# A fifth room for raw weight units, shared with the turning of panels, and four units loaded ahead instead of three, in the MLPs of a two-layer encoder trunk

## The chip, the cores and the metric

The kernel runs on one core of one Trainium2 chip. The metric is device time in microseconds (us) from one launch, the median of several runs; lower is better. The engines are called PE (TensorE, matrix products), ACT (ScalarE), DVE (VectorE), POOL (GpSimd) and SP (SyncE, which here only issues DMAs).

## The reference, cut to what matters

The input x is 256 rows of 2048 floats. Everything is float32. Two layers run one after the other: a layer with causal attention under a forget gate, and a layer with chunked attention on shared keys and values. Each ends in an MLP, and the two MLPs are where the change acts.

```python
def sq_relu_mlp(h, g, w1, w2):
    a = jax.nn.relu(rms_norm(h, g) @ w1)     # w1: 2048 x 8192
    return (a * a) @ w2                      # w2: 8192 x 2048
...
    h = h + o.reshape(B, S, D) @ a_w_out[l]
    h = h + sq_relu_mlp(h, mlp_norm_g[layer], mlp_w1[layer], mlp_w2[layer])
...
kv = rms_norm(h, kv_norm_g) @ kv_w
...
    h = h + o.reshape(B, S, D) @ b_w_out[l]
    h = h + sq_relu_mlp(h, mlp_norm_g[layer], mlp_w1[layer], mlp_w2[layer])
```

## The kernel before

**Products in three passes.** A float32 weight unit of 128 x 1024 is split into two parts that PE takes at its faster format: ACT copies it to `hi` (line 259) and DVE takes `lo = raw - hi` (line 260). The activations are split in the same way. PE then runs three passes over a unit: `hi` with the activations' high part (line 522), `hi` with their low part (line 524), `lo` with their high part (line 526). `hi` and `lo` have three rooms each.

**The loader.** All weight units of the program stand in one deque, `units`, in the order in which they are used. `load()` (line 234) takes the next, gives it a room of the pool `wraw` (four rooms of 128 x 1024, line 93) and issues its DMA of 512 KB on SP (line 242). `issue()` (line 245) takes the oldest loaded unit and writes down its ACT copy and its DVE subtraction. `fetch()` calls `top_up()` (line 274), which keeps two units split ahead of PE (`AHEAD`) and three raw units loaded ahead of the splitting (`EARLY`), and hands the next split unit to the products. So one raw unit loaded follows each raw unit issued, and a load has to wait for the room of the unit loaded four before it, that is, for that unit's `lo`.

**The MLP** is 16 pairs of column blocks in a planned order (`plan_mlp`), blocks of the first product and of the second by turns. A pair of blocks is multiplied by a scheme with seven products of sums of panels in place of eight, over a quarter of the depth for the first pair and over half of it for the 15 others (`deep`). Four panels of a pair (1 MB each in a deep pair) are brought whole by SP (`bring`, line 861). DVE sums some of them (`make`, line 865, its addition at line 879); other sums are made by a DMA of POOL that adds the panel in memory to the panel on the chip (`put`, line 881, its DMA at line 885). A unit made from those panels is called a form; it has no load of its own, passes through the loader's queue as a place holder, and is six matmuls long. A raw unit is twelve matmuls long. A deep pair has 14 forms and 8 raw units; the first pair has 7 forms, 12 raw units and four panels of 512 KB. `prepare` (line 887) decides how many units before a pair each of its panels is brought and summed.

**The turning of panels.** A finished panel of the hidden layer must be turned before it is an operand of the second product. DVE turns its 32 x 32 blocks from the accumulator into a room `z` (`blocks32`, line 369, its instruction at line 372). From there the blocks go to their places either by 16 small DMAs from chip to chip, eight on SP and eight on POOL (`hop`, line 392), or through memory with one DMA out (`turn<-z`, line 382) and four back (line 388; `carry`, line 375). The panels of the residual stream that feed the next normalisation go through `z` as well. `z` comes from the pool `qkv` with two rooms of 128 x 1024 (line 403 in `turned`, two being the pool's number). These z rooms are as large as a room for a raw unit.

**Order.** What is to be done a few units after an event waits in a list, `fill`, of which `run_fill()` takes one place after a unit. At the end `keep_order` (line 70) binds DVE, ACT, PE and SP to the written order; POOL's order is left to the scheduler. So a DMA of SP that waits holds up every later DMA of SP.

Of the kernel before, what the change touches and what calls it, by code (L numbers as in the profile page):

```python
# [9 lines left out]
F32 = mybir.dt.float32  # L10
# [5 lines left out]
P = 128  # L16
# [11 lines left out]
UN = 1024  # L28
# [53 lines left out]
def trunk(ctx: ExitStack, tc: tile.TileContext, xT, xr, gs, hg, bf, wgate, w_in, w_oa, w1a, w1fa, w1sa, w2fa, w2sa,  # L82
# [4 lines left out]
    def pool(name, bufs, **kw):  # L87
        return ctx.enter_context(tc.tile_pool(name=name, bufs=bufs, **kw))
# [4 lines left out]
    wraw = pool("wraw", 4)  # L93
    qkv = pool("qkv", 2)
# [36 lines left out]
    units = deque()  # L131
# [99 lines left out]

    raws = deque()

    def load(parts=1, queue=SY):
        src = units.popleft()
        if isinstance(src, Form):
            raws.append((src, ()))
            return
        raw = wraw.tile([P, UN], F32, name="raw")
        n = UN // parts  # L240
        cuts = [slice(i * n, (i + 1) * n) for i in range(parts)]
        queue.dma_start(raw, src)
        raws.append((raw, cuts))

    def issue(parts=1):
        form = None
        if not raws:
            load(parts)
        raw, cuts = raws.popleft()
        if not cuts:  # L250
            form, half = raw, raw.half
            raw, cuts = form.pair.t[form.name], [slice(0, form.pair.cols - UN if half else UN)]
            if half:
                raw = raw[:, UN:]
        n = cuts[-1].stop
        hi = wsp.tile([P, n], F32R, name="hi" if n == UN else "hih", bufs=3 if n == UN else 1)
        lo = wsp.tile([P, n], F32R, name="lo" if n == UN else "loh", bufs=3 if n == UN else 1)
        for c in cuts:
            S.activation(hi[:, c], raw[:, c], AF.Copy)  # L259
            V.tensor_tensor(lo[:, c], raw[:, c], hi[:, c].bitcast(F32), op=ALU.subtract)  # L260
        ready.append((hi, lo, n < UN))
        if form and form.pair.deep and form.name == "T3":
            make(form.pair, "T2", int(half))
        elif form and half == form.pair.wide:
            if form.name == "T3":
                make(form.pair, "T2")
            elif form.name == "T2" and form.pair.adds:
                put(form.pair, "T4")

    def half_next():  # L270
        u = raws[0][0] if raws else units[0]
        return isinstance(u, Form) and u.half and not u.pair.deep

    def top_up(ahead=AHEAD, early=EARLY):
        while (units or raws) and sum(1 for r in ready if not r[2]) <= ahead and not (half_next() and any(r[2] for r in ready)):
            issue()
        while units and sum(1 for r in raws if r[1]) < early:
            load()

    def fetch(ahead=AHEAD, early=EARLY):  # L280
# [14 lines left out]
    turns = [0]  # L295
# [45 lines left out]
    def room(tag, name, dtype=F32):  # L341
        return qkv.tile([P, DEEP], dtype, name=name, tag=tag, bufs=1)
# [17 lines left out]
    def steps(make):  # L360
        box = []

        def step():
            if not box:
                box.append(make())
            next(box[0])
        return step
# [34 lines left out]
    def turned(name=None):  # L402
        z = qkv.tile([P, GH * T], F32, name="z")
        return (z, qkv.tile([P, GH * T], F32, name=name, tag=name, bufs=2)) if name else z
# [361 lines left out]
    early = room("bias", "early")  # L766
# [127 lines left out]
                (bring if name[0] != "T" else put if p.adds and name == "T1" else make)(p, name)  # L894

    def mlp(plan, x, Sx, st, last, more=None):
        base = turns[0]
        hids = [[] for _ in range(NCH)]
        Sh = [[] for _ in range(NCH)]

        def take(t, c, n):
            S.activation(t, t, AF.Relu)
            y = acts.tile([P, 2, GH, T], F32R, name="act")
            hi, lo = (y[:, i].rearrange("p k (b i c) -> p (k b) i c", b=NB, i=4) for i in range(2))
            t3 = t.rearrange("p (i kb c) -> p kb i c", i=4, c=32)
            yield
            S.activation(hi, t3, AF.Square)
            yield
            S.activation(t, t, AF.Square)
            yield  # L910

            def low():
                V.tensor_tensor(lo, t3, hi.bitcast(F32), op=ALU.subtract)

            hids[c].extend(y[:, :, j, :] for j in range(GH))
            low()
            yield
            if n == 0:
                r = prob.tile([P, 4 * UN], F32R, name="Sh", tag="p", bufs=1)
                Sh[c].extend(r[:, i : i + n] for i, n in ((0, UN), (UN, UN), (2 * UN, UN), (3 * UN, UN)))  # L920
                yield from sums([[t3[:, 2 * j + b :: 4] for j in range(2)] for b in range(NB)], Sh[c])
            elif n == 1:
                yield from sums([[t3[:, 2 * j + b :: 4] for j in range(2)] for b in range(NB)], Sh[c][2:])

        def turn_hidden(c, n):
            zt = []

            def f(b, ps):
                if b == 0:
                    zt.extend(turned("q"))  # L930
                blocks32(ps, zt[0], b)
                if b == NB - 1:
                    step = steps(lambda: take(zt[1], c, n))
                    at = TURNS[c > 0][n]
                    way = [hop(*zt)[0][0]] if at[1] < 0 else [i[0] for i in carry(*zt, 0)[:2]]
                    items = [[] for _ in range(max(at) + 1)]
                    for i, d in zip([i for i in at if i >= 0], way + [step] * (len(at) - 2)):
                        items[i].append(d)
                    add_fill(items)
            return f  # L940

        def open_pair(p):
            second, c, r = p.at
            if c < NCH:
                p.x, p.fs = (hids[c], Sh[c]) if second else (x, Sx)
            p.ps = [acc_pair(base), acc_pair(2 if p.third else 1 - base)]
            if c == NCH:
                p.x, p.fs, evacs = more
                p.evac = evacs[2 * r : 2 * r + 2]
            elif second:  # L950
                p.evac = [(last if c == NCH - 1 else residual)(2 * r + q, st.r2) for q in range(2)]
            else:
                p.evac = [turn_hidden(c, 2 * r + q) for q in range(2)]

        starts = [i for i, it in enumerate(plan) if it[1:] == (2, 0)]
        for i, (p, q, u) in enumerate(plan):
            hi, lo = ready.popleft()[:2] if q > 1 and ready and not p.deep else fetch()
            if p.ps is None:
                open_pair(p)
            f, kind, k = plan[i - 1]  # L960
            done = k if i and kind > 1 and kind == 2 + f.wide else None
            if q > 1:
                form_products(p.ps, hi, lo, p.x, p.fs, u, q == 3, p)
                if u == 1 and q == 2 + p.wide:
                    p.t["P7"] = wk.tile([P, 512], F32, name="p7", tag="wk")
                    S.activation(p.t["P7"], p.ps[1][0], AF.Copy)
                elif u == 2 and q == 2 + p.wide:
                    V.scalar_tensor_tensor(p.ps[0][1], p.ps[1][0], -1.0, p.t["P7"], op0=ALU.mult, op1=ALU.subtract)
                if q == 2 + p.wide:
                    if not p.deep:  # L970
                        top_up(AHEAD - 1)
                    if u == 1:
                        S.activation(p.ps[1][0], p.ps[1][1], AF.Copy, scale=-1.0)
                    if p.deep:
                        run_fill()
            else:
                products(p.ps[q], hi, lo, p.x, u, not units and not ready, p.fast)
                if p.fast and (q, u) == (0, p.own):
                    V.tensor_tensor(p.ps[1][1], p.ps[1][0], p.t["P7"], op=ALU.add)
                run_fill()  # L980
                if u == KT // UA - 1:
                    for b in range(NB):
                        p.evac[q](b, p.ps[q][b])
                nxt = next((j for j in starts if j > i), None)
                if nxt is not None:
                    d = sum(1 for it in plan[i:nxt] if it[1] < 2)
                    prepare(plan[nxt][0], d)
            if done == 1 and not f.adds:
                make(f, "T4")
            elif done == 2:  # L990
                S.activation(f.ps[0][0], f.ps[1][1], AF.Copy)
# [20 lines left out]
    for g in range(NG):  # L1012
# [8 lines left out]
                add_fill([[]] * (9 if g else 7) + [[lambda: qs.append(scale_q(box["lq"], 1, g))]])  # L1021
        evs.append(f)
    mlp(plan_a, x1, S1, st1, next_b, (xb, Sb, evs))
    st2f = st2.flipped

    def rel_bias(g, box):
# [116 lines left out]
```

## Time and profile before

| | |
|---|---|
| median of 3 runs | 2078.71 us (2078.18 to 2079.30) |
| the profiled execution's own time | 2078.09 us |
| its span, first to last instruction | 2076.2 us |
| granted TensorE clock | 1.000 |
| PE busy | 2062.0 us, 99% |
| DVE busy | 1712.5 us, 82% |
| ACT busy | 1313.2 us, 63% |
| POOL busy | 222.9 us, 11% |
| DMA | 543.08 MB, mean 262 GB/s |

The profile is of one execution. Its span lies 1.9 us under that execution's own time. Times inside it are counted from the span's start. Busy is the union of an engine's instructions; matmuls overlap one another in it, since each is given from its start to a modelled end. "A <- B" means that A waited and that B ended last of what it waited for. The first MLP lies at about 400 to 1034 us, the second from about 1405 us to the end; between them are the query, key and value products and the second attention.

### The profile page before, as it was taken

The numbers are of one execution on the slowest core, as the hardware profiler recorded it, in microseconds if no ns is written. First come the engines' busy times: TensorE is split into PE (matmuls) and PEld (weight loads), VectorE is DVE, ScalarE is ACT, GpSimd is POOL, SyncE is SP. The second block draws the span as 40 slices with busy tenths as digits, with TensorE's granted clock in tenths as the row PEclk, the third lists the DMA queues.
The fourth block names the chain that finished last, engine by engine and source line by source line (L and its number), as shares of the span: only waits on it lengthen the run. The fifth ranks groups of instructions, "written<-read, shape, count | busy, mean of one in ns | idle before, by whom it ended". The sixth has DMA issues, their size and how long they took to land.

```text
span 2076.2 us, 26893 instructions
## 1 busy us (share of the span) xinstructions
PE 2062.0 (99%) x9140; PEld 1702.9 (82%) x9140; DVE 1712.5 (82%) x1974; ACT 1313.2 (63%) x1587; POOL 222.9 (11%) x339
## 2 busy tenths in 40 slices
PE   9999999999999999999999999999999999999999
PEld 8888888878878888888878888887788888888887
DVE  6767666799899899899988577768998988998996
ACT  6544444777667677677776445456766776766764
POOL 1111000021101102101011001000211111011020
PEclk9999999999999999999999999999999999999999
DMA  7787778788888898898888777787888888888985
GB/s 287 250 256 237 231 257 263 270 255 270 292 252 279 262 291 281 241 293 271 259 252 273 233 231 237 233 274 270 271 269 278 250 283 288 269 278 258 297 249 174
DMA packets 170682, 543.08 MB, mean 262 GB/s; under 512 B 40480, under 2 KB 68528, under 8 KB 147504
## 3 DMA queue, kind: packets, MB, share of 16 engines
q1 hardware_dynamic: 153008, 463.16, 62.9%
q0 software_dynamic: 17248, 77.64, 18.7%
q8 instruction: 72, 1.18, 0.2%
q10 hardware_dynamic: 288, 0.57, 0.1%
q14 instruction: 66, 0.54, 0.1%
HBM read 501.39 MB, written 26.24 MB: 254 GB/s over the span
## 4 chain that ended last, share of the span: by engine, by line
PE 95%; DMA 3%; ACT 1%; DVE 1%; issue 0%; POOL 0%; ACTq 0%; DVEq 0%; SPq 0%; POOLq 0%
PE acc L526 25%; PE acc L524 25%; PE acc L522 25%; PE s L522 6%; PE s L524 6%; PE s L526 6%; PE s L666 1%; PE po L696 1%; DMA raw<-in_w2sa 1%; DMA wT<-in_w1fa 1%; DMA raw<-in_w2sb 1%; DMA raw<-in_w1b 0%; DMA query<-turn 0%; ACT hi L259 0%; PE po L697 0%; PE s L665 0%
## 5 line engine op out<-in xcount | busy, mean ns | idle before, releaser
L260 DVE TENSOR_TENSOR lo<-raw,hi 128x1024 fp32r<-128x1024 f32 (+1 forms) x514 | 619.7, 1211 | 184.7 <-ACT hi L259 171.3
L259 ACT ACTIVATE hi<-raw 128x1024 fp32r<-128x1024 f32 (+1 forms) x514 | 540.4, 1054 | 341.4 <-PE acc L524 251.4
L522 PE MATMUL acc<-hi,act 128*128 128x512 f32 x2076 | 578.3, 394 | 5.4 <-ACT hi L259 3.4
L526 PE MATMUL acc<-lo,act 128*128 128x512 f32 x2076 | 569.6, 389 | 0.1
L524 PE MATMUL acc<-hi,act 128*128 128x512 f32 x2076 | 569.2, 389 | 0.1
L522 PEld LDWEIGHTS acc<-hi,act 128*128 128x128 f32 x2076 | 387.4, 188 | 85.4 <-ACT hi L259 4.5
L526 PEld LDWEIGHTS acc<-lo,act 128*128 128x128 f32 x2076 | 388.7, 188 | 83.7 <-DVE lo L260 3.4
L524 PEld LDWEIGHTS acc<-hi,act 128*128 128x128 f32 x2076 | 389.4, 188 | 82.6 <-DVE act L353 1.3
L259 ACT ACTIVATE hi<-w 128x1024 fp32r<-128x1024 f32 x258 | 271.1, 1058 | 120.9 <-PE acc L524 105.5
L260 DVE TENSOR_TENSOR lo<-w,hi 128x1024 fp32r<-128x1024 f32 x258 | 310.0, 1217 | 17.4 <-ACT hi L259 16.4
L260 DVE TENSOR_TENSOR lo<-wT,hi 128x1024 fp32r<-128x1024 f32 x184 | 223.2, 1221 | 51.0 <-ACT hi L259 47.5
L259 ACT ACTIVATE hi<-wT 128x1024 fp32r<-128x1024 f32 x184 | 193.3, 1059 | 88.6 <-PE acc L524 34.6
L398 POOL DMA_DIRECT2D q<-z x208 | 103.6, 510 | 259.9 <-DVE z L372 209.6
L522 PE MATMUL s<-hi,act 128*128 128x512 f32 x358 | 98.8, 391 | 3.1 <-ACT hi L259 2.6
L526 PE MATMUL s<-lo,act 128*128 128x512 f32 x358 | 98.6, 390 | 0.0
L524 PE MATMUL s<-hi,act 128*128 128x512 f32 x358 | 98.2, 389 | 0.0
L522 PEld LDWEIGHTS s<-hi,act 128*128 128x128 f32 x358 | 66.8, 188 | 18.4 <-ACT hi L259 3.9
L526 PEld LDWEIGHTS s<-lo,act 128*128 128x128 f32 x358 | 66.9, 188 | 14.6 <-DVE lo L260 0.9
L524 PEld LDWEIGHTS s<-hi,act 128*128 128x128 f32 x358 | 67.2, 188 | 14.1
L879 DVE TENSOR_TENSOR wT<-wT,w 128x1024 f32<-128x1024 f32 x62 | 75.9, 1225 | 2.1
L879 DVE TENSOR_TENSOR wT<-w,w 128x1024 f32<-128x1024 f32 x62 | 75.2, 1214 | 0.3
L608 POOL TENSOR_TENSOR ss<-ss,mhalf 128x4 f32<-128x4 f32 x32 | 43.2, 1357 | 271.0 <-DVE ss L607 270.9
(181 smaller groups left out, 1819.6 us busy)
## 6 DMA issues: line engine op xcount, KB each, us to landing
raw<-in_w_in SPq DMA_DIRECT2D x95, 512.0 KB, 4.5
w<-in_w2fa SPq DMA_DIRECT2D x32, 1024.0 KB, 7.3
raw<-in_w2sa SPq DMA_DIRECT2D x64, 512.0 KB, 6.9
raw<-in_w_kv SPq DMA_DIRECT2D x64, 512.0 KB, 4.4
w<-in_w2fb SPq DMA_DIRECT2D x32, 1024.0 KB, 7.1
raw<-in_w2sb SPq DMA_DIRECT2D x64, 512.0 KB, 6.8
w<-in_w1fa SPq DMA_DIRECT2D x28, 1024.0 KB, 7.4
raw<-in_w1sa SPq DMA_DIRECT2D x56, 512.0 KB, 6.3
```

The lines of the kernel that those rows point to most:

```text
L259: S.activation(hi[:, c], raw[:, c], AF.Copy)
L260: V.tensor_tensor(lo[:, c], raw[:, c], hi[:, c].bitcast(F32), op=ALU.subtract)
L398: (G if i % 2 else SY).dma_start(dst[32 * j : 32 * j + 32, i * n : (i + 1) * n], z[32 * i : 32 * i + 32, j * n : (j + 1) * n])
L522: TE.matmul(ps[:, cols], xh, cut(hi, j), start=first, stop=False, **kw)
L524: TE.matmul(ps[:, cols], xl, cut(hi, j), start=False, stop=False, **kw)
L526: TE.matmul(ps[:, cols], xh, cut(lo, j), start=False, stop=last, **kw)
L608: G.tensor_tensor(rn, vv, mhalf, op=ALU.pow)
L666: TE.matmul(s[:, P : 3 * P], q[:, a, P:T], k[:, a], start=True, stop=True)
L696: TE.matmul(po[:, :T], v[:, 0, a * P : (a + 1) * P], pT[:, :2], start=True, stop=False)
L879: V.tensor_tensor(d, a, b, op=ALU.add)
```

## The change

While an MLP runs, `extra[0]` is true. Then every fifth raw unit (counted over the whole program in `extra[1]`) gets one of the two rooms of `z` in place of a room of `wraw`, and `top_up` keeps four raw units loaded ahead in place of three. In the first MLP this ends when the products that follow the MLP are opened; in the second it lasts to the end. The number of rooms in each pool, the order of the units, their sizes, the splitting, the products and the turning are as before.

```diff
+    extra = [False, 0]
+
     def load(parts=1, queue=SY):
         src = units.popleft()
         if isinstance(src, Form):
             raws.append((src, ()))
             return
-        raw = wraw.tile([P, UN], F32, name="raw")
+        extra[1] += 1
+        raw = qkv.tile([P, UN], F32, name="zraw", tag="z", bufs=2) if extra[0] and extra[1] % 5 == 0 else wraw.tile([P, UN], F32, name="raw")
...
     def top_up(ahead=AHEAD, early=EARLY):
...
-        while units and sum(1 for r in raws if r[1]) < early:
+        while units and sum(1 for r in raws if r[1]) < early + extra[0]:
             load()
...
     def mlp(plan, x, Sx, st, last, more=None):
-        base = turns[0]
+        base, extra[0] = turns[0], True
...
             if c == NCH:
+                extra[0] = False
                 p.x, p.fs, evacs = more
...
     mlp(plan_a, x1, S1, st1, next_b, (xb, Sb, evs))
+    extra[0] = False
```

## The prediction

> **What bounds the kernel now.** I read the page first: the span, the engines, and the transfers of raw units.
>
> ```profile
> span 2076.2 us, 26893 instructions
> PE 2062.0 (99%) x9140; PEld 1702.9 (82%) x9140; DVE 1712.5 (82%) x1974; ACT 1313.2 (63%) x1587; POOL 222.9 (11%) x339
> ```
>
> PE is busy for all but 2076.2 - 2062.0 = 14.2 us. No loader can give more than that. So the question is what PE waits for in these 14 us. The second view is PE's waits: who, for what, us in total, times, longest.
>
> ```profile
> PE acc L522 <- ACT hi L259: 3.4, 3, 1.3
> PE s L522 <- ACT hi L259: 2.6, 2, 2.4
> PE acc L522 <- ACT act L352: 2.0, 2, 1.4
> ```
>
> PE waits a handful of times, almost always for ACT. ACT itself is idle a third of the time, so the third view is what ACT's splitting (L259) waits for when it is a DMA.
>
> ```profile
> ACT hi L259 <- DMA wT<-in_w1fa: 9.3, 5, 3.1
> ACT hi L259 <- DMA wT<-in_w1fb: 7.9, 3, 2.9
> ACT hi L259 <- DMA raw<-in_w2sa: 6.7, 4, 4.8
> ACT hi L259 <- DMA raw<-in_w1b: 4.8, 1, 4.8
> ```
>
> Two kinds are in the MLPs: late raw units (the third and fourth row), and sums that POOL's DMA makes (`wT`, 5 + 3 = 8 waits in these rows). The change reaches only the first kind. PE is covered by two units split ahead, so only the longest waits get through. The two of 4.8 us do. I followed both in the timelines and the chain.
>
> **First place, 587 us**, in the first MLP: PE's timeline, ACT's, the chain, and SP's (start, length, engine, what, count).
>
> ```profile
> 584.70 0.61 PE L526 MATMUL acc<-lo,act 128*128 128x512 f32 x2
> 587.70 1.19 PE L522 MATMUL s<-hi,act 128*128 128x512 f32 x4 [2.38 <-ACT hi L259]
> ```
> ```profile
> 586.59 1.06 ACT L259 ACTIVATE hi<-raw 128x1024 fp32r<-128x1024 f32 x1 [4.82 <-DMA raw<-in_w2sa]
> ...
> 591.49 1.05 ACT L259 ACTIVATE hi<-raw 128x1024 fp32r<-128x1024 f32 x1
> ```
> ```profile
> 574.04 12.45 DMA raw<-in_w2sa
> ```
> ```profile
> 563.84 0.47 SPq L242 DMA_DIRECT2D raw<-in_w2sa  x1
> 570.48 1.75 SPq L388 DMA_DIRECT2D q<-turn  x4
> 573.64 0.35 SPq L863 DMA_DIRECT2D w<-in_w1fa  x1
> 574.04 2.21 SPq L242 DMA_DIRECT2D raw<-in_w2sa  x3
> ```
>
> SP issued a raw load at 563.84, then stood before the four DMAs of a turned panel and a bring, and came to the next load only at 574.04. It took 12.45 us and landed at 586.49. PE, which could have gone on at about 585.15 (584.70 and two starts 0.23 apart), stood until 587.70.
>
> **Second place, 1441 us**, at the start of the second MLP.
>
> ```profile
> 1440.12 1.07 PE L526 MATMUL acc<-lo,act 128*128 128x512 f32 x4
> 1441.78 1.19 PE L522 MATMUL acc<-hi,act 128*128 128x512 f32 x4 [0.59 <-ACT act L352]
> 1443.04 1.20 PE L524 MATMUL acc<-hi,act 128*128 128x512 f32 x4
> 1444.07 1.08 PE L526 MATMUL acc<-lo,act 128*128 128x512 f32 x4
> ```
> ```profile
> 1433.12 0.89 ACT L349 ACTIVATE y<-q,gsb 128x256 f32<-128x256 f32 x2
> 1438.78 1.06 ACT L259 ACTIVATE hi<-raw 128x1024 fp32r<-128x1024 f32 x1 [4.76 <-DMA raw<-in_w1b]
> 1439.74 0.90 ACT L349 ACTIVATE y<-q,gsb 128x256 f32<-128x256 f32 x2
> 1440.67 1.06 ACT L352 ACTIVATE act<-y 128x1024 fp32r<-128x1024 f32 x1
> ```
> ```profile
> 1425.75 0.33 SPq L242 DMA_DIRECT2D raw<-in_w1b  x1
> ...
> 1430.30 1.24 SPq L242 DMA_DIRECT2D raw<-in_w1b  x2
> ```
>
> The raw load of 1430.30 lands at 1438.7. ACT works in written order, so behind this unit stand the last two scalings and the copy of the activations (L352), and PE waits for those.
>
> **The change part by part.** *Four ahead.* A load is written one raw unit earlier. Today the load behind the issue of unit j brings unit j+3, afterwards j+4. The counts per kind, the sizes and the places of the loads among SP's other DMAs stay; each place carries the next unit. *The fifth room.* With four rooms unit j+3 waits for the `lo` of unit j-1. With five, unit j+4 waits for that same `lo`. So SP waits at the same instants as today, and what is queued behind it (brings, turned panels, the hops) is not held longer. Without the fifth room it would wait for the `lo` of unit j, just written, and hold them all. No instruction is added; one load in five takes a z room.
>
> At the first place, then, the late unit is carried by the load of 563.84. This is the row of the DMA view for that single load, the us to landing last.
>
> ```profile
> raw<-in_w2sa SPq DMA_DIRECT2D x1, 512.0 KB, 11.9
> ```
>
> It lands at 563.84 + 11.9 = 575.7, some 8 us before ACT must start on it (585.15 less ACT's 1.06). The wait of 587.70 - 585.15 = 2.55 us goes, and with it the slow start behind it (0.12 us: four matmuls in 588.73 - 587.70 = 1.03 us, where 0.91 is usual). Gain 2.67 us. What is late next? The unit after it, today the second of the three loads from 574.04, would be carried at 574.04 and land at 586.5. ACT takes it at 591.49 today, at about 589 without the stall. So 2.5 us are left, and the gain should stand.
>
> At the second place the late unit is carried at 1425.75. The DMA view of that load:
>
> ```profile
> raw<-in_w1b SPq DMA_DIRECT2D x1, 512.0 KB, 4.2
> ```
>
> It lands near 1430. ACT can then go on from 1434.0 (1433.12 + 0.89) instead of 1438.78. From there to the end of L352 it needs 2.95 us, so that ends near 1437, or a little later if a room of `hi` is not free at once, before PE comes to it at 1441.03. PE's three passes start 0.75, 0.35 and 0.12 us late today (1441.78 for 1441.03; 1.26 and 1.03 us apart for 0.91). Gain 1.22 us. The unit after it is carried at 1430.30, lands at 1438.7, and is needed at 1441 or later.
>
> Two costs. *The extra load* on entering each MLP, one more transfer of 512 KB where none was, is nothing on the path: it falls where `EARLY` units are in hand, and one unit less is loaded at the end. *A z room taken by a raw unit*: when such a load falls between two turned panels of a pair, the second panel takes the room of the first, and DVE must wait until the first has been read. Least time between two such panels, and the hop that reads the first one:
>
> ```profile
> 418.19 1.30 DVE L372 STREAM_TRANSPOSE z<-acc 128x512 f32<-128x512 f32 x2
> ...
> 433.35 1.30 DVE L372 STREAM_TRANSPOSE z<-s 128x512 f32<-128x512 f32 x2
> ```
> ```profile
> L398 POOL DMA_DIRECT2D q<-z x8: 498/498/542, 420.1 to 426.1; - x8
> ...
> DMA to landing us min/median/max: 3.7/5.1/6.1
> ```
>
> The panels are 15.2 us apart. The hop's last DMA is issued at 426.1 and none of its 16 takes over 6.1 us, so the room is free by 432.2, before DVE needs it. Price nothing; if the hop were 5 us longer, DVE would wait up to 4 us there, and PE for an accumulator. Between these ends I take nothing, by the row.
>
> **The sum.** 2.67 + 1.22 = 3.89 us. On the profiled execution, whose own time is 2078.09 (1.9 around the span), that is 2074.2; it stands 0.6 under the median of the runs. From the median: 2078.71 - 3.89 = 2074.8.
>
> **Rivals.**
>
> *More goes.* PE's three rows of waits sum to 8.0 us, of which the two places are 2.38 + 0.59 = 2.97. If earlier raw units take some burden off the other 5.0 us too, say half of them, the time is 2078.71 - 3.89 - 2.5 = 2072.3. Against it: the bytes per time are the same.
>
> *The stall moves.* At 574.04 SP issued three loads in 2.21 us without a room to wait for; its own order was late. If the burst only moves to the next unit (2.5 us are left there), or a load into z waits for a hop and holds SP just there, the first gain is lost and the second stays: 2078.71 - 1.22 = 2077.5.
>
> *The rooms are not the shortage.* The change then does not do what it says: units come no sooner where it matters, because SP's order and the transfer set the landing, and the time stays at 2078.7. For it: the late load had no room to wait for, and the two late raw units stand 850 us apart. Against it: the place in SP's order moves as well. The Trainium skill, in Perfetto Trace Analysis, section Optimization Strategy, says that the same gap repeating for a stretch can mean that there is no room for the next tile; by that sign, which is missing here, rooms are not short.
>
> *Slower: sums behind loads.* A sum of POOL and the raw load beside it share the transfer:
>
> ```profile
> 429.36 11.91 DMA wT<-in_w1fa
> ```
> ```profile
> wT<-in_w1fa POOLq DMA_DIRECT2D x7, 1024.0 KB, 10.3
> ```
>
> This sum took 11.91 us where the median is 10.3, and PE stood behind it at 442 us. If one more load lies beside each sum, it lands later by the load's share, 0.52 MB at the mean of 262 GB/s or 2.0 us. ACT already waits for 8 of them; each that passes its delay to PE costs 2.0. With all 8 the cost is 16 us and the time 2090.8; with five, 2078.71 - 3.89 + 10 = 2084.8. From two on nothing is gained, from five on it is a loss over 0.2% (8.1 us). Against it: loads follow issues one for one, so nothing is added beside a sum, only another unit. The Trainium skill, in DMA: Bandwidth & Descriptors, section Issuing engines are not separate DMA queues, says that DMAs of SP, ACT and POOL run on the same 16 DMA engines and interleave. The row of 11.91 agrees with that.
>
> **How the numbers follow.** A measurement of this kernel can tell about 0.2%, 4.2 us, from no change; the bounds are 2074.55 and 2082.87. The forecast gets 0.60, more goes 0.10, the moved stall 0.10, rooms not short 0.05, slower 0.15. The forecast's 3.89 lies just inside the bound. Runs scatter by 1.1 us and POOL's order may be scheduled anew, so I give its case 0.26 beyond the bound and 0.34 within. Faster 0.26 + 0.10 = 0.36; within 0.34 + 0.10 + 0.05 = 0.49; slower 0.15. The range leaves out the slow case and the far part of "more goes": 2071.5 to 2079.5.
>
> **What would show it.** ACT's waits for `raw<-in_w2sa` and `raw<-in_w1b` fall from 6.7 and 4.8 us to near nothing; ACT's waits for `wT` and PE's waits behind them stay. PE's row at about 585 follows without a gap. SP's waits for `lo` and the landing times stay as they are. Wrong would be: DVE's L372 waiting for a DMA, a raw load of SP waiting for a hop, `wT` landing later than 10.3 in the median, or a new PE wait after 587.

## The result and the profile after

The changed kernel takes 2070.85 us in the median of 8 executions (2069.23 to 2076.18), the kernel before 2078.44 (8 executions, 2075.64 to 2080.47). The ratio is 0.9965, interval 0.9952 to 0.9978: faster, by 7.6 us. The forecast was 3.9 us, and the time lies 0.65 us under its range. The profiled execution took 2071.0 us at a granted clock of 1.000. In the lines below, L522, L524 and L526 of the kernel before are L525, L527 and L529, L259 and L260 are L262 and L263, L242 is L245.

From the page of the changed kernel: the span, the engines, and the copies out of the rooms that are shared with the turning.

```profile
span 2068.8 us, 26858 instructions
...
PE 2060.2 (100%) x9140; PEld 1705.4 (82%) x9140; DVE 1713.6 (83%) x1974; ACT 1314.4 (64%) x1587; POOL 223.9 (11%) x339
...
L262 ACT ACTIVATE hi<-zraw 128x1024 fp32r<-128x1024 f32 x53 | 56.0, 1056 | 30.9 <-PE acc L527 25.3
```

The work is the same: 9140 matmuls, and every engine's busy time within 3 us. 53 raw units went through a z room. The span is 7.4 us shorter: 5.6 of them are time in which PE is not busy (2068.8 - 2060.2 = 8.6 us where it was 14.2), the other 1.8 are in PE's busy time itself. PE's waits in the changed kernel (for whom, us in total, times, longest):

```profile
PE acc L525 <- ACT hi L262: 2.0, 2, 1.1
PE pt L123 <- DVE mhalf L125: 1.1, 1, 1.1
PE acc L525 <- ACT act L355: 0.7, 1, 0.7
```

Of the three rows of before (3.4, 2.6 and 2.0 us) 2.0 and 0.7 are left. Now the two places of the forecast, in PE's timeline of the changed kernel:

```profile
583.01 0.62 PE L529 MATMUL acc<-lo,act 128*128 128x512 f32 x2
583.47 1.07 PE L525 MATMUL s<-hi,act 128*128 128x512 f32 x4
...
1436.41 1.07 PE L525 MATMUL acc<-hi,act 128*128 128x512 f32 x4
1437.31 1.07 PE L527 MATMUL acc<-hi,act 128*128 128x512 f32 x4
```

Both gaps are gone: the starts follow at 0.46 and 0.90 us, as two and four matmuls do. SP's timeline shows how the unit needed at 583.5 was carried:

```profile
561.59 1.15 SPq L245 DMA_DIRECT2D zraw<-in_w2sa  x1
567.36 1.75 SPq L391 DMA_DIRECT2D q<-turn  x4
571.96 0.35 SPq L866 DMA_DIRECT2D w<-in_w1fa  x1
572.36 0.91 SPq L245 DMA_DIRECT2D raw<-in_w2sa  x2
```

It was loaded at 561.59, into a z room, ahead of the turned panel's four DMAs, and no longer behind them.

**Where the time went, matmul by matmul.** Both programs run the same 9140 matmuls in the same order, so the start of matmul n in one trace can be set against its start in the other. The changed kernel loses 1.2 us in its first thirty matmuls (a slow clock; the last section has it), and from there it gains: 0.9 us from 412 to 427, 1.7 at 442 to 444, 0.4 to 557, 2.7 at 587, 0.3 in small steps to 1073, 1.2 at 1441, 0.7 to 1459, 0.8 to 1522, less 0.3 from there to the end, 8.4 in all. So the two terms of the sum came out as forecast, 2.7 for 2.67 and 1.2 for 1.22. The other 4.5 us come from places that were not in the sum.

**One of these had been in the trace under another name.** The ACT timeline of the kernel before, at the start of the first MLP:

```profile
407.06 1.06 ACT L259 ACTIVATE hi<-raw 128x1024 fp32r<-128x1024 f32 x1 [3.64 <-PE s L524]
```

The wait of 3.64 us is put down to a matmul of PE. But the DMA view of the load that SP issued at 399.47 reads:

```profile
raw<-in_w1a SPq DMA_DIRECT2D x1, 512.0 KB, 7.5
```

399.47 + 7.5 = 406.97, and ACT starts at 407.06: this unit was late too. It does not stand in the row of ACT's waits for `raw`. The same stretch of the changed kernel:

```profile
405.51 1.06 ACT L262 ACTIVATE hi<-raw 128x1024 fp32r<-128x1024 f32 x1 [0.86 <-PE acc L527]
```

Here ACT waits for PE alone (0.86 us), which needs it no sooner.

### The profile page after: what moved, and what is told of

Read it like the earlier page. It is cut to its first block, busy times and chain, and to the rows that moved or that the text cites. A ratio compares the mean times of both kernels' runs of the same rounds, so it can differ in the third digit from the quotient of the medians.

```text
span 2068.8 us, 26858 instructions
## 1 busy us (share of the span) xinstructions
PE 2060.2 (100%) x9140; PEld 1705.4 (82%) x9140; DVE 1713.6 (83%) x1974; ACT 1314.4 (64%) x1587; POOL 223.9 (11%) x339
## 4 chain that ended last, share of the span: by engine, by line
PE 98%; DMA 1%; ACT 0%; DVE 0%; POOL 0%; issue 0%; ACTq 0%; DVEq 0%; POOLq 0%
PE acc L529 26%; PE acc L525 26%; PE acc L527 26%; PE s L525 7%; PE s L529 7%; PE s L527 6%; PE s L669 1%; PE po L699 1%; DMA query<-turn 0%; PE s L668 0%; PE po L700 0%; DMA turn<-z 0%; DMA raw<-in_w_in 0%; PE s L792 0%; ACT hi L262 0%; POOL query L391 0%
## 5 line engine op out<-in xcount | busy, mean ns | idle before, releaser
L263 DVE TENSOR_TENSOR lo<-raw,hi 128x1024 fp32r<-128x1024 f32 (+1 forms) x461 | 555.9, 1211 | 164.7 <-ACT hi L262 151.9
L262 ACT ACTIVATE hi<-raw 128x1024 fp32r<-128x1024 f32 (+1 forms) x461 | 484.8, 1054 | 293.5 <-PE acc L527 228.2
L525 PE MATMUL acc<-hi,act 128*128 128x512 f32 x2076 | 578.9, 394 | 2.8 <-ACT hi L262 2.0
L529 PE MATMUL acc<-lo,act 128*128 128x512 f32 x2076 | 569.6, 389 | 0.1
L527 PE MATMUL acc<-hi,act 128*128 128x512 f32 x2076 | 569.4, 389 | 0.1
L527 PEld LDWEIGHTS acc<-hi,act 128*128 128x128 f32 x2076 | 389.9, 188 | 82.2 <-DVE act L356 0.5
L529 PEld LDWEIGHTS acc<-lo,act 128*128 128x128 f32 x2076 | 389.4, 188 | 82.4 <-DVE lo L263 1.6
L525 PEld LDWEIGHTS acc<-hi,act 128*128 128x128 f32 x2076 | 388.1, 188 | 82.4 <-ACT hi L262 2.8
L262 ACT ACTIVATE hi<-w 128x1024 fp32r<-128x1024 f32 x258 | 271.2, 1058 | 132.4 <-PE acc L527 111.2
L263 DVE TENSOR_TENSOR lo<-w,hi 128x1024 fp32r<-128x1024 f32 x258 | 309.9, 1217 | 16.5 <-ACT hi L262 15.3
L263 DVE TENSOR_TENSOR lo<-wT,hi 128x1024 fp32r<-128x1024 f32 x184 | 223.4, 1221 | 53.4 <-ACT hi L262 50.3
L262 ACT ACTIVATE hi<-wT 128x1024 fp32r<-128x1024 f32 x184 | 193.7, 1059 | 87.1 <-PE acc L527 35.9
L525 PE MATMUL s<-hi,act 128*128 128x512 f32 x358 | 98.4, 390 | 0.5 <-DVE s L983 0.5
L527 PE MATMUL s<-hi,act 128*128 128x512 f32 x358 | 98.2, 389 | 0.0
L529 PE MATMUL s<-lo,act 128*128 128x512 f32 x358 | 98.2, 389 | 0.0
L525 PEld LDWEIGHTS s<-hi,act 128*128 128x128 f32 x358 | 67.0, 188 | 14.6 <-issue 0.9
L527 PEld LDWEIGHTS s<-hi,act 128*128 128x128 f32 x358 | 67.2, 188 | 14.0
L529 PEld LDWEIGHTS s<-lo,act 128*128 128x128 f32 x358 | 67.2, 188 | 14.0
L262 ACT ACTIVATE hi<-zraw 128x1024 fp32r<-128x1024 f32 x53 | 56.0, 1056 | 30.9 <-PE acc L527 25.3
```

The lines of the kernel that those rows point to most:

```text
L525: TE.matmul(ps[:, cols], xh, cut(hi, j), start=first, stop=False, **kw)
L527: TE.matmul(ps[:, cols], xl, cut(hi, j), start=False, stop=False, **kw)
L529: TE.matmul(ps[:, cols], xh, cut(lo, j), start=False, stop=last, **kw)
```

## The experiments

**The theories.** A: the room is what matters; SP held for an old room brings units too late, and more ahead only needs the room. B, from the forecast: four ahead is what matters, and the room only keeps SP from being held. And for the gain that was not in the sum, two places were suspects: the start of each MLP, and places like the one at 587 us, which differ from execution to execution.

One measure serves all runs: the time lost in a stretch is the time between the starts of its first and last matmul, less 0.2267 us (the pace at which matmuls follow one another without a gap) for each matmul between. The stretches are cut at the same matmuls in every trace, and named by their time in the changed kernel. "Six places" are those where a panel is turned through memory while a deep pair is brought, near 587, 754, 917, 1617, 1780 and 1943 us, each taken from some 22 us before that time to 12 us behind it. The measure is from profiled executions, one number for each; the times below are of many executions.

| us lost | 400-430 | 430-455 | 455-500 | six places | 1400-1465 | 1465-1530 |
|---|---|---|---|---|---|---|
| before, three traces | 0.9, 0.8, 0.8 | 1.8, 2.4, 2.1 | 0.6, 1.4, 1.5 | 2.7, 3.1, 8.4 | 2.0, 1.3, 2.4 | 3.0, 2.2, 4.1 |
| the change, two traces | 0.0, 0.0 | 0.1, 2.3 | 0.4, 0.4 | 0.0, 0.1 | 0.0, 0.0 | 2.1, 2.2 |
| room only, three traces | 0.0, 0.0, 0.0 | 0.0, 0.0, 0.0 | 0.4, 0.4, 0.4 | 8.6, 4.0, 3.3 | 0.0, 0.3, 0.0 | 0.5, 2.9, 2.5 |
| four ahead only | 1.6 | 1.3 | 4.0 | 0.1 | 2.2 | 7.7 |
| change at the start only | 0.0 | 0.0 | 0.4 | 5.0 | 0.0 | 2.1 |
| change after the start | 0.8 | 1.1 | 2.7 | 0.1 | 0.0 | 4.5 |
| the same, entered on a z room | 0.7 | 1.2 | 0.4 | 0.1 | 0.6 | 4.1 |
| before, small DMAs (7) | 0.3 | 2.6 | 0.7 | 11.0 | 0.3 | 3.3 |
| the change, one sum later (8) | 0.0 | 1.2 | 1.3 | 0.1 | 0.0 | 2.2 |

**1. The room without the fourth unit.** Edit of the changed kernel:

```diff
-        while units and sum(1 for r in raws if r[1]) < early + extra[0]:
+        while units and sum(1 for r in raws if r[1]) < early:
```

> The fifth room stays, but three units are loaded ahead as before. Theory (units land late because their loads stand late in SP's written order; the room only keeps SP from waiting): the late unit of 587 us is still carried by the load that SP reaches after the turned panel, so the stalls at 587 and 1441 stay and the time is within 2 us of the kernel before (ratio 0.999 to 1.001). Rival (rooms were the shortage): most of the 7.6 us is gained, ratio below 0.9975.

Measured: 2071.77 us in the median of 12 executions (2068.89 to 2077.64), 0.9968 of before, interval 0.9955 to 0.9981. This missed B's number: the room alone gains 6.6 us, not to be told from the whole change. The largest row of SP's waits, that of its raw loads, in the kernel before and with the room alone:

```profile
SPq L242 <- DVE lo L260: 659.5, 289, 6.2
```
```profile
SPq L245 <- DVE lo L263: 403.4, 213, 6.7
```

With four rooms the load written behind the issue of unit j has to wait for the `lo` of unit j-1; with five and three ahead it needs only that of j-2. The raw loads' waits for `lo` fall by 256 us. SP as a whole does not wait less: the waits of the brings and of the small DMAs behind grow by as much, and all of SP's waits come to 1482 us where they were 1493. But the raw loads start sooner: measured by the matmul that PE has come to, those of the MLPs are issued 2.1 us sooner in the mean, and in the changed kernel 5.1 us sooner. The table shows what that does: the losses at 400 to 455 and at 1400 to 1465 are gone, and those at the six places are not. PE's timeline in its profiled execution (2077.64 us, the slowest of the 12):

```profile
583.70 0.61 PE L529 MATMUL acc<-lo,act 128*128 128x512 f32 x2
586.90 1.21 PE L525 MATMUL s<-hi,act 128*128 128x512 f32 x4 [2.59 <-ACT hi L262]
587.95 1.80 PE L527 MATMUL s<-hi,act 128*128 128x512 f32 x4
...
754.28 1.21 PE L525 MATMUL s<-hi,act 128*128 128x512 f32 x4 [2.12 <-ACT hi L262]
```

The stall at 587 is there as before, and another at 754.

**2. Four ahead without the room.** Edit of the changed kernel:

```diff
-        raw = qkv.tile([P, UN], F32, name="zraw", tag="z", bufs=2) if extra[0] and extra[1] % 5 == 0 else wraw.tile([P, UN], F32, name="raw")
+        raw = wraw.tile([P, UN], F32, name="raw")
```

> Four units ahead in the four old rooms, no z room. Theory: a load now waits for the lo that was written just before it and SP is held by it, with brings, hops and turned panels behind it. The late raw units go as in the changed kernel, but part of the gain is given back: between 3 us faster and 5 us slower than the kernel before (ratio 0.9985 to 1.0025), and SP's waits of raw loads for lo grow above the 660 us of before. Rival (order alone does it, SP's waiting is free): the full gain, ratio 0.9965.

Measured: 2089.81 us (6 executions, 2087.01 to 2091.24), 1.0051 (1.0036 to 1.0067). Slower, and by more than was expected. The same row of SP's waits, and PE's waits:

```profile
SPq L245 <- DVE lo L263: 1005.6, 353, 7.8
```
```profile
PE s L529 <- DVE lo L263: 3.7, 3, 1.4
PE acc L525 <- ACT hi L262: 3.6, 3, 2.8
PE s L525 <- ACT hi L262: 3.4, 2, 2.1
```

A load now waits for a `lo` just written. Its row is 346 us above that of the kernel before, while all of SP's waits rise by 9 us only (1502): SP reaches what stands behind the loads so late that these have less to wait for. 4.0 us are lost at 455 to 500 and 7.7 at 1465 to 1530. But the six places lose nothing. So the two parts do different things: four ahead covers the six places, the room pays for it and clears the starts of the MLPs.

**3. The change in the first pair of each MLP only.** Edit of the changed kernel, where a pair is opened:

```diff
+            if p.deep:
+                extra[0] = False
```

> Four ahead and z rooms only from the entry of each MLP until its first deep pair is opened; afterwards three ahead and four rooms. Theory of a cascade (one late unit near 407 us puts ACT, DVE and the hops behind, and the waits at 418 to 444 us follow from it; likewise at 1438 to 1459 us): the waits at 418 to 444 and at 1441 to 1459 us are gone although the loads beside the sum at 429 us are as before, the stall at 587 us stays; gain 3.5 to 5 us, ratio 0.9976 to 0.9983. Rival (the sum lands sooner because the loads beside it are moved): the wait at 442 us stays, gain about 1 to 2 us, ratio 0.999 or more.

Measured: 2074.6 us (12 executions), 0.9981 (0.9970 to 0.9991), as expected. The starts of both MLPs lose nothing (0.0 in three columns), the six places are as in the kernel before. In this execution it was the last that stalled:

```profile
1934.85 0.61 PE L529 MATMUL acc<-lo,act 128*128 128x512 f32 x2
1938.21 1.76 PE L525 MATMUL s<-hi,act 128*128 128x512 f32 x4 [2.74 <-ACT hi L262]
1939.76 1.91 PE L527 MATMUL s<-hi,act 128*128 128x512 f32 x4
```

**4. The change from the first deep pair on.** Edit of the changed kernel, in `mlp` and where a pair is opened:

```diff
-        base, extra[0] = turns[0], True
+        base, extra[0] = turns[0], False
...
+            if p.deep:
+                extra[0] = True
```

> The other part: the old loader until the first deep pair of each MLP is opened, four ahead and z rooms from then on. Theory of the cascade: the waits at 407 to 444 and at 1441 to 1459 us stay as in the kernel before, those at 587 and 1522 us go; gain 2.7 to 3.5 us, ratio 0.9983 to 0.9987. Rival (loads beside the sum): the wait at 442 us goes here, gain over 4.5 us.

Measured: 2077.26 us (12 executions), 0.9996 (0.9984 to 1.0008): a miss. The six places are covered, but the switch itself costs. The fourth unit is loaded at once, while the next z room is up to four loads away, so for these SP should stand as in experiment 2 (experiment 5 puts this to the test). The stretch from 1400 to 1465 was expected to lose as before and lost nothing, though the loader there is the old one. PE now waits where it did not before:

```profile
454.75 0.73 PE L529 MATMUL acc<-lo,S 128*128 128x512 f32 x2 [0.60 <-DVE lo L263]
461.95 0.74 PE L529 MATMUL s<-lo,act 128*128 128x512 f32 x2 [1.39 <-DVE lo L263]
```

**5. The same, but the fourth unit starts with a load that gets a z room.** Edit, beside that of 4, with a third place in `extra` that says that the deep pairs have begun:

```diff
         extra[1] += 1
+        extra[0] = extra[0] or extra[2] and extra[1] % 5 == 0
```

> The old loader at the entry of each MLP; after the first deep pair is opened, four ahead and z rooms, begun at a load that gets a z room, so that SP is not held by the lo just written. Theory: the waits around 407 to 444 and 1441 to 1459 us stay, all six places where a panel goes through memory have over 4 us of slack; gain 3 to 4.5 us, ratio 0.9978 to 0.9986, and no loss at 456 to 462 us as with the earlier kernel that began there without a z room. Rival (only the entry matters): ratio 0.9995 or more.

Measured: 2075.71 us (12 executions), 0.9988 (0.9975 to 1.0001); it just missed, and the interval reaches no change. The loss at 455 to 500 is 0.4 us in place of 2.7, which bears out the cause given for that loss in 4 (one trace each). Of the six places the first two have 2.2 and 2.0 us to spare, not over 4. Late units at the start stay: ACT waits 3.4 us for one in each MLP. Experiments 3 and 5 add to 0.0019 + 0.0012 = 0.0031, against 0.0035 for the whole, each with an interval of 0.001 or more to either side.

**6. Does the place differ from execution to execution?** The kernel before, unchanged, profiled again.

> The kernel before, unchanged, profiled once more. Theory now (six like places, where a panel goes through memory and SP comes late to a burst of loads; each has 0.1 to 1.5 us of slack in the traces so far, and how many of them stall PE differs from execution to execution): the stalls at the start of the MLPs (442, 1441 and 1474 us) come again, but the stall of 587 us may be absent there or stand at one of 754, 917, 1617, 1780 or 1938 us. If the stall of 587 us is a fixed property of that place alone, it comes again there and nowhere else.

It does. PE's timeline in this execution (2080.4 us), at 587, 754 and 1943 us:

```profile
588.05 0.61 PE L526 MATMUL acc<-lo,act 128*128 128x512 f32 x2
588.53 1.19 PE L522 MATMUL s<-hi,act 128*128 128x512 f32 x4
...
751.56 0.61 PE L526 MATMUL acc<-lo,act 128*128 128x512 f32 x2
752.86 1.20 PE L522 MATMUL s<-hi,act 128*128 128x512 f32 x4 [0.69 <-ACT hi L259]
...
1943.88 0.61 PE L526 MATMUL acc<-lo,act 128*128 128x512 f32 x2
1945.83 1.20 PE L522 MATMUL s<-hi,act 128*128 128x512 f32 x4 [1.33 <-ACT hi L259]
```

The stall of 2.38 us at 587 that carried the forecast is not there, and two others are. At all six places SP stands before the four DMAs of a turned panel, then brings a panel, then issues three raw loads close together; PE's stalls are behind the first of these. The DMA view of that load at the place near 1943 us, in the first trace of before (no stall) and in this one (stall):

```profile
raw<-in_w2sb SPq DMA_DIRECT2D x1, 512.0 KB, 6.4
```
```profile
raw<-in_w2sb SPq DMA_DIRECT2D x1, 512.0 KB, 11.4
```

Seven traces have the panel turned through memory and three units ahead in the deep pairs (before, room alone, and the start only). In 26 of their 42 cases this load landed in 6.2 to 7.2 us, and ACT never waited for it. In the 16 others it took 7.7 to 13.3 us and ACT waited; in the 12 of these with 10.7 us or more PE stalled. All 16 stand at three of the six places: 587 (every trace), 754 (four) and 1943 (five). At 917, 1617 and 1780 us no trace shows a late unit. So the six share SP's order, which leaves little to spare, and how long one load takes decides whether PE stalls. In the first trace of before, the tightest unit of the three loads at each of the five places that did not stall landed 0.84, 1.21, 1.17, 0.41 and 1.30 us before ACT took it. In the changed kernel the six are 3.3 to 7.6 us, in both of its traces.

**7. The turned panel by small DMAs in place of the way through memory.** Edit of the kernel before, in the table of turns, which takes the four DMAs out of SP's way:

```diff
-     (0, 2, 8, 10, 10, 14, 18, 20, 22),
+     (0, -1, 8, 10, 10, 14, 18, 20, 22),
```

> The kernel before, with the second panel of a later pair turned by 16 small chip-to-chip DMAs instead of going out to memory and back. Theory: at the six places SP no longer stands before the four DMAs that bring the panel back, so the loads behind it start 3 to 6 us sooner and the late units there go with the old loader; gain 2.5 to 4.5 us, ratio 0.9978 to 0.9988, if the hops cost nothing. Rival (the transfer's length, not SP's order, makes the units late): no gain, ratio 0.9995 or more.

Measured: 2085.68 us (11 executions), 1.0040 (1.0024 to 1.0056): a miss. The six places lose 11.0 us in place of 2.7 to 8.4. The small DMAs have waits of their own on SP (near 587 us they stand 5.1 us for a panel that is being brought), so the edit did not take SP's order away and is no test of it. It shows one thing all the same: at all six places a raw unit is late that takes only 5.6 to 7.1 us to land, so here it is the late issue and not a long transfer.

**8. The changed kernel with one sum later.** In both traces of the changed kernel PE still waits at about 1467 us for a sum that POOL's DMA makes:

```profile
1467.62 0.73 PE L525 MATMUL acc<-hi,act 128*128 128x512 f32 x2 [1.14 <-ACT hi L262]
```

The order of the forms of that pair was changed, so that this sum is used one unit later:

```diff
-    "ahead1": "a4 F F a5 a6 a7 F b4",
+    "ahead1": "a4 F a5 F a6 a7 F b4",
```

> The changed kernel, and in the pairs of the first product's second half the raw unit a5 stands before the second form, so that the form that waits for POOL's second sum comes 2.7 us later. Theory: the wait of 1.1 us and its slow starts at 1467 us (1.75 us) go, nothing else moves: 2069.1, ratio to the kernel before 0.9957, 0.9992 of the changed kernel. Rival: the units moved ahead make another wait; 2071 or more.

Measured: 2072.99 us (11 executions), 0.9979 (0.9969 to 0.9988): no better than the change, and in the rival's range. The wait moves to a form that now comes sooner:

```profile
1472.65 1.20 PE L525 MATMUL acc<-hi,act 128*128 128x512 f32 x4 [1.50 <-ACT hi L262]
```

**9. Four more traces,** on one chip: the room alone twice, the kernel before and the changed kernel once each.

> The kernel with the fifth room alone, profiled once more. Its one trace so far stalls at 587 and 754 us and was the slowest of its 12 executions. If a room alone also helps at the six places (SP is held one lo less, so the loads behind the turned panel start sooner), this trace shows none or one of the six stalls and a time of 2069 to 2073 us; if it helps only at the entry of the MLPs, stalls at the six places come as often as in the kernel before and the time is about 2074.6, that of the kernel with the change at the entry alone.

> As the run before it: the fifth room alone, one more execution, to see how the six places differ between executions.

> The kernel before once more. Theory: late raw units at the entry (near 407 and 1438 us) again, and another choice of the six places stalls PE; each has under 1.5 us of slack between landing and use.

> The changed kernel once more. Theory: no raw unit of an MLP lands late, the six places have over 2 us of slack each, PE waits for ACT in the MLPs only behind POOL's sums; 2069 to 2072 us.

Measured: room alone 2075.11 and 2075.63 us, before 2088.14, the change 2073.85 (over its expected range). The room alone stalls at two of the six places in each trace (1.68 us at 587 and 1.51 at 1943; 1.35 at 587 and 1.09 at 754), before at two (3.15 and 1.54), the change at none. So the room alone does not keep PE from stalling there, and as its two traces are of one kernel on one chip, the places differ by execution and not only by chip. Over all traces the six places split cleanly: 2.7 us or more are lost in the eight traces in which deep pairs load three ahead (before, room alone, the start only, and experiment 7), 0.1 or less in the six in which they load four ahead. One thing spoke against the change's credit: in its second trace PE waits again at 442 us.

```profile
443.47 0.73 PE L525 MATMUL acc<-hi,act 128*128 128x512 f32 x2 [1.61 <-ACT hi L262]
```

There the sum that POOL's DMA makes from about 429 us took 12.7 us; it took 10.5 in the first trace of the change, 8.1 to 10.0 in the four traces that have the room at the start and three units ahead in the deep pairs, and 11.9 to 12.6 in the three of before. In experiment 8, with the change's loader, it took 11.8, and 1.2 us are lost. So the 1.7 us gained at 430 to 455 between the first two traces hang on this sum as well, and are not the change's for certain.

## Why the prediction had the two places right and the sum too small

**What PE waits for: right.** The 14 us outside PE's busy time were the right place to look, and late raw units were a part of them. "No loader can give more than that" is not quite so: 1.8 us of the gain lie in PE's busy time, in matmuls that start slowly behind a stall.

**The two terms: right, for this pair of executions.** 2.7 us for 2.67, and 1.2 for 1.22, with the units carried as foretold: the load at 561.59 in place of 563.84, landing 11.4 us later where 11.9 were assumed. That each came out so well is in part luck. In the second trace of before PE does not stall at 587 us, and with the old loader at the start of the second MLP experiments 4, 5 and 7 lose 0.0, 0.6 and 0.3 us from 1400 to 1465, where the traces of before lose 1.3 to 2.4.

**The sum, "2.67 + 1.22 = 3.89 us": this is the step that failed.** It priced two waits of one execution, where the change acts on classes of places. The first class is the six places: which of them stall differs from execution to execution (with the old way of turning only 587, 754 and 1943 us were seen to), and what they lose in the traces of before is 2.7, 3.1 and 8.4 us. The forecast had the smallest of these and took it for the whole. The second class is the start of an MLP: 2.6 to 3.2 us are lost at 400 to 455 and 1.3 to 2.4 at 1400 to 1465, of which the sum had 1.22. The unit at 407 us was missed because the row of ACT's waits names one releaser and here named PE, and no load was set against it. "More goes" was the right rival, with 0.10 of the chances and 2.5 us beyond the sum; measured are 7.6 - 3.9 = 3.7.

**"SP waits at the same instants as today": nearly.** The changed kernel's row is this:

```profile
SPq L245 <- DVE lo L263: 643.4, 267, 9.0
```

It was 659.5 in 289 waits. Experiment 2 shows the condition on which it rests: without the room it is 1005.6.

**"The fifth room only keeps SP from being held", and so gains nothing alone: wrong.** This step took four ahead to be the gain. Experiment 1 gave 0.9968 for the room alone. With three ahead the room lets each load wait for a `lo` one issue older, and this moves loads forward as well, by 2.1 us in the mean. "Rooms are not the shortage" fell with it. It had leaned on the Trainium skill, Perfetto Trace Analysis, section Optimization Strategy, by which a gap that repeats hints at missing room. Here rooms were short, and no gap repeated in the trace that was read; the six places show over several executions only, with 0.41 to 1.30 us to spare in the first trace at those that did not stall.

**The costs taken as nothing: right.** In the changed kernel DVE's turning into `z` waits for PE alone (5.1 us in 6 waits, as before), and SP's raw loads wait 1.4 us in all for DMAs out of `z`. "Slower: sums behind loads" did not happen; ACT's waits for `wT` from the first product, 9.3 and 7.9 us before, are now:

```profile
ACT hi L262 <- DMA wT<-in_w1fa: 5.2, 3, 3.2
ACT hi L262 <- DMA wT<-in_w1fb: 3.5, 2, 2.8
```

That they would stay was wrong, to the good side here; those of the second product's sums went from 5.7 to 7.3 us.

**What stays open.** How much time the fourth unit adds. By the times, room alone and the whole change are the same (0.9968 and 0.9965, intervals that overlap). By the traces they are not alike: in each of the three of the room alone, ACT takes 11 or 12 raw units of the MLPs within 0.2 us of their landing (10 to 16 in before), in the two of the change one, and the room alone still loses 3.3 to 8.6 us at the six places. But the three profiled executions of it (2075.1 to 2077.6 us) are slower than the median of the 12, so the traces may show it from its worse side. Why the first raw load of three lands in 6.4 us in one execution and in 12 in another, at the same place, was not tried.

## What to carry to other kernels

A gap in one trace stands for a class of places: look for every place in the code with the same order of DMAs, read how many microseconds each has to spare there, and price the class, not the gap that this execution happened to show. Set each long wait of a splitting engine against the landing of the load that it reads, whatever name the wait bears. Give a deeper prefetch a room of its own: the depth without the room cost 0.5% here, the room without the depth gained 0.3% but left about as many units late as before.

## What the runs showed of the hardware that was not expected

A stall of PE can cost more than its gap. In the third trace of before, PE's timeline behind the stall at 593 us:

```profile
593.11 2.07 PE L522 MATMUL s<-hi,act 128*128 128x512 f32 x4 [3.15 <-ACT hi L259]
594.98 1.91 PE L524 MATMUL s<-hi,act 128*128 128x512 f32 x4
596.68 1.91 PE L526 MATMUL s<-lo,act 128*128 128x512 f32 x4
```

The four matmuls that begin at 594.98 take 1.7 us to the next group (596.68) where 0.91 is usual, 0.43 us each in place of 0.23. This lasts for 14 matmuls and costs 3.0 us beyond the gap. The trace shows why: TensorE's granted clock was halved there. A row of this view gives a stretch, its length, each engine's busy time, the granted clock, the DMA share and GB/s; the first is behind this stall, the second behind that of 587 us in the first trace of before:

```profile
592.40:599.20 6.80, 6.09 (x14) 4.79 (x15) 6.05 (x6) 5.55 (x6) 0.00 (x0) 0.50 0.36 137
```
```profile
587.70:591.10 3.40, 3.40 (x15) 2.83 (x16) 3.37 (x3) 3.37 (x4) 0.00 (x0) 1.00 0.65 246
```

One stretch of 3.4 us at 0.50, at a cost of 1.7 us each, follows the gaps of 2.59 and 2.12 us in experiment 1, of 2.74 in experiment 3 and of 1.97 in experiment 5 at 1469 us. None follows the gap of 2.38 at 587 us in the first trace of before, nor that of 1.68 in a trace of the room alone, so the length of the gap does not settle it. Where the gap lies does, as far as the 14 traces go. The clock changes on a grid: in the trace of experiment 1 it changes at 588.1, 591.5, 755.3 and 758.7 us, and the 167.2 us from the first to the third are 49 times 3.41. In all 13 grid stretches in which PE was idle for 1.9 us or more, the next one was at 0.50; of the eight with 1.5 to 1.7 us of idle time one was followed so. The gap of 2.38 us is cut by the grid into 0.75 and 1.64 us. No run was made to test this reading, and two cases do not fit it: the second half of the 6.8 us above (0.7 us of idle time in the stretch before it, at the half clock), and the changed kernel's beginning.

That beginning has the same spacing, behind a gap of 0.90 us:

```profile
7.01 1.22 PE L525 MATMUL acc<-hi,act 128*128 128x512 f32 x2 [0.90 <-ACT hi L262]
8.03 1.05 PE L527 MATMUL acc<-hi,act 128*128 128x512 f32 x2
```

This is most of what it loses there; its trace has no record of the clock before 10.4 us. The Trainium skill, TensorE: Matmul & The Clock Gate, section Part 1: The HAM clock gate, describes half the clock after an idle window of about 3.4 us, with starts 426.7 ns apart for 512 columns. The spacing of 0.43 agrees; the gaps behind which it was seen here, 0.9 to 3.2 us, are shorter.

The times of whole executions follow the granted clock too: in 29 executions of before, those at 1.000 had a mean of 2076.5 us (10 of them), those at 0.999 2079.0 (15), those at 0.998 2081.8 (3). That is no cause beside the stalls: in the traces a lower mean clock is made of such stretches (0.999 with one of them, 0.998 with two or three, 0.996 with four), and these stand behind stalls, or at the program's start, where the change does nothing. Of the changed kernel's 8 executions 6 were at 1.000, with a mean of 2070.5, 6 us under those of before; but the two groups did not run side by side.
